# A hybrid attention and convolution block on one core: the conv result split behind the keys, its mean one block later, branch weights in pairs, branch groups in the attention's ramp, and the last tile in halves

## The chip, the cores and the metric

The kernel runs on one core of a Trainium2 chip. The metric is the device time of one execution in microseconds (us). TensorE (PE) does the matmuls, VectorE (DVE) and ScalarE (ACT) the elementwise work, GpSimd (POOL) some of it too, and SyncE (SP) issues the DMAs from one in-order queue.

## The reference, cut to what matters

Sequence 1024, model width 1024, float32, one layer.

```python
proj = rms_norm(x, norm_in_g) @ w_in
q, k, v, z_a, q_idx, k_idx, w_idx, glu_in, z_b, gate_a, gate_b = split(proj)
attn = sparse_attention(q, k, v, q_idx, k_idx, w_idx, rel_bias)   # top 256 keys of each query, 8 heads
y_a = (attn * silu(z_a)) @ w_branch_a
u = glu_in[:, :512] * sigmoid(glu_in[:, 512:])
c = silu(layer_norm(causal_depthwise_conv(u, conv_w, conv_b)))    # 31 taps
y_b = (c * silu(z_b)) @ w_branch_b
x = x + (sigmoid(gate_a) * y_a + sigmoid(gate_b) * y_b) @ w_out
x = x + sigmoid(rms_norm(x, ple_norm_g) @ w_ple_gate) * (p @ w_ple_proj)
out = rms_norm(x, final_norm_g)
```

## The kernel before

**Precision.** Every matmul operand is split into a high part and a low part (`hi`, `lo`), and `mm3` (L195) does three matmuls for each pair of operands (L199, L200, L201). A weight goes through `load_w` (L160): one DMA on SP into a `raw` buffer of 1024 words per partition (L173), a cast on ACT into `hi` (L177), a subtract on POOL into `lo` (L178). A weight with a per-row gain takes L182 and L183 instead. The value weights are 256 columns wide, so that one half of V takes two such loads.

**Order.** The program is written as a straight line, and a planner that simulates a timeline fixes each engine's order before the run. `hp()` raises an instruction's priority; `issue_after(i)` puts an instruction behind `i` on the engine of `i`. Buffers come from pools on a left and a right stack of SBUF; a pool that opens where an older one lay waits for that one's readers, tile by tile.

**Stages, in order.** The input is normalized and transposed into `hTh`, `hTl` (pool `h`). GLU, indexer scores (`wide`), then blocks of gate projections: `gate` (L455) runs, for each 128 columns of weight, two halves of 24 matmuls, an activation (L462) and a store (L463). Beside these, DVE does the conv taps (L295) and, with ACT, a bit search for each query's 256th score (L425 to L450), and then the masks (L506 to L521). The conv result `A[0..3]` gets a layer norm: a matmul with ones for the mean (L588), four gate blocks, a matmul for the variance (L601), then L604 to L618. After the masks `A` is split into `Yh` (ACT, L628) and `Yl` (DVE, L629), and pool `u`, which holds `A`, is closed. Four more gate blocks, `queries(m)` and `keys(m)` for m = 0 to 3 follow (each ends in stores of the split result to DRAM: L555, L556, L566, L567), then V: two halves c of 256 columns, eight tiles of 24 matmuls of 256 columns, evacuated by L650 and L651 into `VC`. The weights of half 0 come through pool `w3`, those of half 1 through pool `w`.

**Attention.** For each of 8 heads and 4 query pairs j: `scores` (matmuls L713, L714; mask add and row maximum on DVE, L721; exponential on ACT, L724), and two steps behind it `values` (transposes L773 to L781, split L784 and L785, matmuls L734). After every one of the 80 groups in `values`, `fill` may run one of 64 steps of `branch_b` (three matmuls of 512 columns, L812 to L814, all into PSUM bank 3; after every fourth a multiply, L817): the step of number n runs from group 4 + 1.25 n on. Branch b's weights come in single blocks of 128 columns through pool `wq` (three buffers of 512 words), which opens when V has ended.

**Last stages.** The merge (L860 to L874) multiplies the attention result by `w_branch_a`, block by block; the output projection takes `w_out` through pool `w2`; then the gate of the per-layer embedding (L947 to L960), the sums for the last norm (L962 to L968) and `final` (L935), which scales a tile in two halves (L938) and stores them (L939).

Of the kernel before, what the change touches and what calls it, by code (L numbers as in the profile page):

```python
# [38 lines left out]
def hybrid_block(ctx: ExitStack, tc: tile.TileContext, x, p, norm_in_g, w_in, conv_w, conv_b,  # L39
# [117 lines left out]

    wpools, wn = [WP], [0]

    def load_w(src, cols, nk_=NK, g=None, pool=None, prio=True):  # L160
# [428 lines left out]
    gate(C_SA, d_sa, 4, AF.Sigmoid)  # L589
# [51 lines left out]
    for c in range(2):  # L641
        w = load_w(win, [(C_V + 256 * c, 256)], pool=(WX, WP)[c])
# [50 lines left out]

    def scores(h, j, head):
# [4 lines left out]
        for i in (2 * j, 2 * j + 1):  # L699
# [10 lines left out]
            for a, b in pieces.get(n, ((0, n),)):  # L710
# [3 lines left out]
                nc.tensor.matmul(L, q_, kl[:, a:b], start=False, stop=True)  # L714
# [14 lines left out]
    FILL0, FILL1, PIN = 4, 1.25, True  # L729
# [65 lines left out]

    def branch_b():
        for m in range(8):
            for a in (m, m + 1):
                if a == 8:
                    waq[0] = load_w(wba, [(0, 128)], 4)  # L800
                elif a not in wbq:
                    wbq[a] = load_w(wbb, [(128 * a, 128)], 4)
            for hf in range(2):
# [4 lines left out]
                for k in range(4):  # L808
                    wh, wl = wbq[m][0][k], wbq[m][1][k]
                    pin = tc.issue_after(last_pe[0].ins) if PIN and last_pe[0] is not None else nullcontext()  # L810
                    with pin:
# [14 lines left out]
    def fill():  # L826
        while done[1] < 64 and done[0] >= FILL0 + FILL1 * done[1]:
# [32 lines left out]
    for m in range(8):  # L860
        wa = waq[m] if m in waq else load_w(wba, [(128 * m, 128)], 4)
# [3 lines left out]
        for hf in range(2):  # L865
# [3 lines left out]
            mm3(o, cut(wa, 0, 128), [(AH[k][:, sl], AL[k][:, sl]) for k in range(4)])  # L869
# [35 lines left out]
    for c in range(2):  # L905
        w = load_w(wo, [(512 * c, 512)], pool=W2)
# [123 lines left out]
```

## Time and profile before

| | us |
|---|---|
| median of three runs (1031.3 to 1032.18) | 1031.77 |
| the profiled execution | 1031.0 |
| its span, first to last instruction | 1029.1 |
| PE busy in the span | 998.2 (97%) |
| DVE, ACT, POOL busy | 714.7, 516.5, 277.3 |

PE is busy for nearly the whole span, but a busy PE isn't always PE at its higher clock: the granted clock says which of its two levels it had. The profiled execution took 1.9 us more than its span, and 0.77 us less than the median.

### The profile page before, as it was taken

To read this page: it belongs to the slowest core of one execution; us is meant where nothing else is said; L and a number is where in the kernel's file an instruction comes from. 1 tells how busy PE (TensorE), PEld (TensorE's weight loads), DVE (VectorE), ACT (ScalarE), POOL (GpSimd) and SP (SyncE) were. 2 spreads that over 40 slices of the span, in tenths; PEclk is the share of its full clock that TensorE was granted. 3 is DMA by queue.
4 is the path that set the end of the run, shared out by engine and by line. 5 is a ranking of instruction groups with operands and counts; after the bars stand their busy time and mean duration, and the time that the engine had idled before them with its cause. 6 is when DMAs were issued, how large, how long until landed. Compare 5 with 4: busy or idle time off the path is not lost.

```text
span 1029.1 us, 13977 instructions
## 1 busy us (share of the span) xinstructions
PE 998.2 (97%) x4993; PEld 835.3 (81%) x4993; DVE 714.7 (69%) x1418; ACT 516.5 (50%) x976; POOL 277.3 (27%) x260
## 2 busy tenths in 40 slices
PE   7999999999999999999997989999999999999996
PEld 6778888888888868788886979888888788888885
DVE  4396455899999999999795149898866922342443
ACT  7344444465665677776623157676643302351321
POOL 5231102321323111242204033444413713100011
PEclk9999999999999999999998999999999999999998
DMA  7240201142223242232447355565229552020012
GB/s 245 59 143 21 62 21 42 52 122 82 90 85 113 82 143 82 83 103 79 112 115 239 93 141 158 153 189 160 83 88 358 181 201 82 1 82 1 21 62 102
DMA packets 95203, 111.44 MB, mean 108 GB/s; under 512 B 6340, under 2 KB 64764, under 8 KB 95134
## 3 DMA queue, kind: packets, MB, share of 16 engines
q1 hardware_dynamic: 95134, 110.56, 35.3%
q8 instruction: 39, 0.64, 0.3%
q14 instruction: 30, 0.25, 0.1%
HBM read 81.16 MB, written 30.95 MB: 109 GB/s over the span
## 4 chain that ended last, share of the span: by engine, by line
PE 53%; DVE 35%; ACT 4%; issue 3%; DMA 3%; SPq 1%; POOL 0%; DVEq 0%; POOLq 0%; ACTq 0%
DVE acc L295 13%; PE bank L199 13%; PE bank L201 13%; PE bank L200 12%; PE bank L734 3%; DVE i_j L447 3%; DVE c_t L435 2%; DVE c_k L434 2%; DVE u_u L295 2%; ACT i_aj L429 2%; PE bank L773 2%; PE wide L371 1%; PE wide L372 1%; DMA w_raw<-in_w_in_dram 1%; PE bank L812 1%
## 5 line engine op out<-in xcount | busy, mean ns | idle before, releaser
L199 PE MATMUL bank<-h_h,w_hi 128*128 128x512 f32 (+2 forms) x720 | 279.8, 389 | 3.2 <-ACT s_g L281 1.2
L200 PE MATMUL bank<-h_l,w_hi 128*128 128x512 f32 (+2 forms) x720 | 278.4, 387 | 0.0
L201 PE MATMUL bank<-h_h,w_lo 128*128 128x512 f32 (+2 forms) x720 | 277.8, 386 | 0.0
L178 POOL TENSOR_TENSOR w_lo<-w_raw,w_hi 128x1024 fp32r<-128x1024 f32 (+1 forms) x57 | 141.6, 2487 | 353.2 <-ACT w_hi L177 344.9
L429 ACT ACTIVATE i_aj<-i_S,c_d 128x384 bf16<-128x384 f32 (+3 forms) x150 | 124.4, 829 | 79.1 <-DVE c_d L425 60.5
L199 PEld LDWEIGHTS bank<-h_h,w_hi 128*128 128x128 f32 (+1 forms) x720 | 134.9, 187 | 32.8 <-ACT s_g L281 1.6
L200 PEld LDWEIGHTS bank<-h_l,w_hi 128*128 128x128 f32 (+1 forms) x720 | 135.0, 188 | 28.0 <-issue 1.1
L201 PEld LDWEIGHTS bank<-h_h,w_lo 128*128 128x128 f32 (+1 forms) x720 | 134.9, 187 | 28.1 <-issue 1.2
L295 DVE SCALAR_TENSOR_TENSOR acc<-u_u,c_c,acc 128x1024 f32<-128x1024 f32 x100 | 128.7, 1287 | 2.4
L199 PE MATMUL bank<-w_hi,g_h 128*128 128x512 f32 x256 | 100.2, 393 | 0.0
L200 PE MATMUL bank<-w_lo,g_h 128*128 128x512 f32 x256 | 100.0, 393 | 0.0
L201 PE MATMUL bank<-w_hi,g_l 128*128 128x512 f32 x256 | 100.0, 391 | 0.0
L177 ACT CAST w_hi<-w_raw 128x1024 fp32r<-128x1024 f32 (+1 forms) x57 | 59.0, 1038 | 73.4 <-PE bank L201 28.3
L380 DVE SCALAR_TENSOR_TENSOR i_S<-wide,c_c,i_S 128x384 f32<-128x384 f32 (+5 forms) x42 | 39.4, 950 | 42.4 <-ACT wide L376 42.2
L704 POOL TENSOR_TENSOR e_mt<-m_m,ea_tp 128x256 f32<-128x256 bf16 (+1 forms) x64 | 41.1, 651 | 87.4 <-DVE c_c L721 73.4
L376 ACT ACTIVATE wide<-wide 128x384 f32<-128x384 f32 (+5 forms) x48 | 35.3, 743 | 47.4 <-PE wide L372 44.5
L199 PEld LDWEIGHTS bank<-w_hi,g_h 128*128 128x128 f32 x256 | 48.1, 188 | 9.8
L201 PEld LDWEIGHTS bank<-w_hi,g_l 128*128 128x128 f32 x256 | 48.1, 188 | 9.7
L200 PEld LDWEIGHTS bank<-w_lo,g_h 128*128 128x128 f32 x256 | 48.1, 188 | 9.7
L724 ACT ACTIVATE e_P<-e_P,c_c 128x384 f32<-128x384 f32 (+4 forms) x64 | 49.6, 776 | 11.0 <-DVE c_c L721 10.5
L959 DVE TENSOR_TENSOR s_g<-bank,s_g 128x512 f32<-128x512 f32 (+1 forms) x17 | 11.2, 661 | 63.0 <-ACT s_g L958 63.0
L199 PE MATMUL bank<-w_hi,h_h 128*128 128x256 f32 x128 | 37.1, 293 | 6.8 <-ACT w_hi L177 6.7
(239 smaller groups left out, 1920.4 us busy)
## 6 DMA issues: line engine op xcount, KB each, us to landing
w_raw<-in_w_in_dram SPq DMA_DIRECT2D x48, 512.0 KB, 4.1
x_x<-in_x_dram SPq DMA_DIRECT2D x8, 512.0 KB, 4.8
s_g<-d_sb SPq DMA_DIRECT2D x16, 256.0 KB, 4.7
ea_st<-d_q SPq DMA_DIRECT2D x8, 512.0 KB, 4.2
d_yb<-s_g SPq DMA_DIRECT2D x16, 256.0 KB, 2.1
f_sa<-d_sa SPq DMA_DIRECT2D x8, 512.0 KB, 5.7
f_yb<-d_yb SPq DMA_DIRECT2D x8, 512.0 KB, 6.8
w_raw<-in_w_out_dram SPq DMA_DIRECT2D x8, 512.0 KB, 3.8
```

What stands on the lines that cost most here:

```text
L177: nc.scalar.copy(hi, raw)
L178: nc.gpsimd.tensor_tensor(lo, raw, f(hi), op=OP.subtract)
L199: nc.tensor.matmul(o, lh, rh, start=(k == 0), stop=False)
L200: nc.tensor.matmul(o, lh, rl, start=False, stop=False)
L201: last_mm[0] = nc.tensor.matmul(o, ll, rh, start=False, stop=(k == n - 1))
L295: return nc.vector.scalar_tensor_tensor(o_, U[c][:, j:j + 1024], ccol[:, c, j:j + 1], i_, OP.mult, OP.add)
L376: nc.scalar.activation(d, d, AF.Relu)
L380: last_score = nc.vector.scalar_tensor_tensor(s_, d, wc, s_, OP.mult, OP.add)
L429: nc.scalar.activation(ajunk[:, :nblk[i]], sblk(i), AF.Sign, bias=f(cand)[:, i - 2:i - 1], accum_out=cnt[:, i - 2:i - 1])
L447: nc.vector.tensor_scalar(junk[:, :nblk[i]], sblk(i), f(cand)[:, i - 2:i - 1], 0.0, OP.is_ge, OP.add, accum_out=cnt[:, i - 2:i - 1])
L704: nc.gpsimd.tensor_tensor(mt, MK[:, moff[i] + n - wl:moff[i] + n], tp[:, 256 - wl:256], op=OP.add)
L724: nc.scalar.activation(P, P, AF.Exp, bias=init, scale=-1.0, accum_out=sm[:, c3])
```

## The change

The branch is the same arithmetic in another order.

1. **Mean one block later.** Gate block 0 of `C_SA` now stands ahead of the mean's matmul, and blocks 1 to 4 between mean and variance; blocks 5 to 7 follow later.
2. **Conv result split behind the keys.** `Yh` and `Yl` are made after the last key's evacuation, and pool `u` is closed there. Ahead of it the weights of V's half 0 are loaded, now through pool `w`; those of half 1 come through `w3`.
3. **Pool `w` is kept** to the end, at a place below `h`, with one `raw` buffer instead of two. Pool `wq` is gone. Branch weights come in pairs: 256 columns, 1024 words. The first two pairs are loaded ahead of the attention.
4. **Ramp.** In head 0 three, three, two and two steps of `branch_b` follow the scores of j = 0 to 3; the rest starts at group 6 with 1.2 groups to a step, so that the 64th comes with group 70 of 80.
5. **Merge.** Branch a's pairs 2 and 3 are loaded at m = 2 and m = 4, and the first load of `w_out` is put behind the last of them on POOL and SP.
6. **Last tile.** The 24 matmuls of the last tile become 24 of 256 columns for each half. The final gain is multiplied in early, the last sum is on DVE, the scale runs on ACT and DVE, one half each, and ACT issues one of the two stores. Squares are scaled by 1/32 inside the activation.

```diff
+RD = 1.0 / 32.0
+    WP = Pool("w", [("raw", 1024, 1), ("hi", 1024, 2), ("lo", 1024, 2)])
     HP = Pool("h", [("h0", 4096, 1), ("h1", 4096, 1), ("l0", 4096, 1), ("l1", 4096, 1)])
-    WP = Pool("w", [("raw", 1024, 2), ("hi", 1024, 2), ("lo", 1024, 2)])
...
     next_gate()
+    gate(C_SA, d_sa, 1, AF.Sigmoid)
     with hp(), tc.issue_after(last_mm[0].ins):
         for hf, sl, z0, z1, z2 in halves():
             nc.vector.tensor_tensor(z0, z0, A[3][:, sl], op=OP.add)
             nc.tensor.matmul(st[hf], ones, z0, start=True, stop=True)
-    gate(C_SA, d_sa, 4, AF.Sigmoid)
+    gate(C_SA, d_sa, 5, AF.Sigmoid, 1)
...
-    for c in range(4):
-        nc.scalar.copy(Yh[c], A[c])
-        nc.vector.tensor_tensor(Yl[c], A[c], f(Yh[c]), op=OP.subtract)
-    UP.close()
-    gate(C_SA, d_sa, 8, AF.Sigmoid, 4)
+    gate(C_SA, d_sa, 8, AF.Sigmoid, 5)
     for m in range(4):
         queries(m)
     for m in range(4):
         keys(m)
+    wv = load_w(win, [(C_V, 256)], pool=WP)
+    with tc.issue_after(last_kv[0].ins), tc.issue_after(last_kv[1].ins):
+        for c in range(4):
+            nc.scalar.copy(Yh[c], A[c])
+            nc.vector.tensor_tensor(Yl[c], A[c], f(Yh[c]), op=OP.subtract)
+    UP.close()
...
-        w = load_w(win, [(C_V + 256 * c, 256)], pool=(WX, WP)[c])
+        w = load_w(win, [(C_V + 256 * c, 256)], pool=WX) if c else wv
...
-    WP.close()
     HP.close()
-    WQ = Pool("wq", [("raw", 512, 3), ("hi", 512, 3), ("lo", 512, 3)])
-    wpools[0:] = [WQ]
+    wpools[0:] = [WP]
...
-    FILL0, FILL1, PIN = 4, 1.25, True
+    FILL0, FILL1 = 6, 1.2
+    RAMP = (3, 3, 2, 2)
...
+    def wb_load(q):
+        if q < 4:
+            wbq[q] = load_w(wbb, [(256 * q, 256)], 4)
+        else:
+            waq[q - 4] = load_w(wba, [(256 * (q - 4), 256)], 4)
+    wb_load(0)
+    wb_load(1)
...
+                        if c0 and hf:
+                            wb_load(q + 2)
...
-        while done[1] < 64 and done[0] >= FILL0 + FILL1 * done[1]:
+        while done[1] < 64 and done[0] >= FILL0 + FILL1 * (done[1] - sum(RAMP)):
...
             todo.append((h, j) + scores(h, j, head) + (ao,))
+            if h == 0:
+                for _ in range(RAMP[j]):
+                    next(fills)
+                done[1] += RAMP[j]
...
     for m in range(8):
-        wa = waq[m] if m in waq else load_w(wba, [(128 * m, 128)], 4)
+        if m in (2, 4):
+            wb_load(5 + m // 2)
+        wa = waq[m // 2]
...
     for c in range(2):
-        w = load_w(wo, [(512 * c, 512)], pool=W2)
+        with tc.issue_after(last_lo[0].ins) if c == 0 else nullcontext(), tc.issue_after(last_dma[0].ins) if c == 0 else nullcontext():
+            w = load_w(wo, [(512 * c, 512)], pool=W2)
...
-            nc.vector.scalar_tensor_tensor(o_, o_, r3[:, t:t + 1], FG[:, a:a + 512], OP.mult, OP.mult)
-            nc.sync.dma_start(out2d[t * 128:(t + 1) * 128, a:a + 512], o_)
+            if t < 7:
+                nc.vector.scalar_tensor_tensor(o_, o_, r3[:, t:t + 1], FG[:, a:a + 512], OP.mult, OP.mult)
+            elif a == 0:
+                nc.scalar.activation(o_, o_, AF.Copy, scale=r3[:, t:t + 1])
+            else:
+                nc.vector.tensor_scalar(o_, o_, r3[:, t:t + 1], None, OP.mult)
+            (nc.sync if t < 7 or a else nc.scalar).dma_start(out2d[t * 128:(t + 1) * 128, a:a + 512], o_)
...
-            mm3(o, mcut(t), cut(w, 0, 512))
...
+                if tail:
+                    o = bank((eb - 1 + a // part) % 8)
+                mm3(o[:, cc], mcut(t), cut(w, a, part))
...
+                if tail and a == 0:
+                    nc.vector.tensor_tensor(X2[:, t, 0:x0 + part], X2[:, t, 0:x0 + part], FG[:, 0:x0 + part], op=OP.mult)
...
-                nc.gpsimd.tensor_scalar(r3[:, t1], rx[:, t1], 1.0 / D, r2b[:, t1], OP.mult, OP.add)
+                nc.vector.tensor_scalar(r3[:, t1], rx[:, t1], r2b[:, t1], None, OP.add)
                 nc.gpsimd.tensor_tensor(r3[:, t1], r3[:, t1], nhalf, op=OP.pow)
+                if tail:
+                    nc.vector.tensor_tensor(xs, xs, FG[:, 768:1024], op=OP.mult)
```

## Rows read from the trace of the kernel before

**Rows 1.** The waits of PE over the whole span: who waited for whom, us in total, how often, the longest.
```profile
PE bank L199 <- ACT w_hi L177: 7.5, 2, 6.7
PE bank L588 <- DVE u_u L587: 2.5, 1, 2.5
PE bank L201 <- POOL wq_lo L178: 2.2, 1, 2.2
PE bank L734 <- ACT e_pth L784: 1.3, 1, 1.3
```

**Rows 2.** Busy time of each engine in slices of 25 us: an ordinary gate slice and two in which the granted clock (PEclk) falls. The columns are start:end, length, and busy us (instructions) of PE, PEld, DVE, ACT and POOL, then PEclk, DMA share and GB/s.
```profile
225.00:250.00 25.00, 25.00 (x112) 20.69 (x111) 24.37 (x26) 15.20 (x30) 6.04 (x3) 1.00 0.31 95
...
350.00:375.00 25.00, 22.52 (x89) 16.94 (x88) 24.05 (x49) 17.85 (x38) 5.81 (x3) 0.93 0.28 84
...
550.00:575.00 25.00, 18.27 (x137) 18.07 (x136) 5.38 (x11) 5.42 (x11) 4.93 (x3) 0.86 0.59 196
```

**Rows 3.** PE in order of time around the mean's and the variance's matmul: start, duration, operation. Matmuls overlap, so the pace is read from the starts.
```profile
364.25 0.39 PE L201 MATMUL bank<-h_h,w_lo 128*128 128x512 f32 x1
367.12 3.41 PE L588 MATMUL bank<-u_u,c_c 128*128 128x512 f32 x4 [2.48 <-DVE u_u L587]
...
370.75 0.49 PE L200 MATMUL bank<-h_l,w_hi 128*128 128x512 f32 x1
...
414.20 1.88 PE L601 MATMUL bank<-u_u,c_c 128*128 128x512 f32 x4
...
416.15 0.40 PE L200 MATMUL bank<-h_l,w_hi 128*128 128x512 f32 x1
```

**Rows 4.** DVE, POOL, SP and ACT in order of time between the split of the conv result and V's weights.
```profile
538.66 1.22 DVE L629 TENSOR_TENSOR y_y<-u_u,y_y 128x1024 fp32r<-128x1024 f32 x1
540.40 7.87 DVE L629 TENSOR_TENSOR y_y<-u_u,y_y 128x1024 fp32r<-128x1024 f32 x3
...
541.43 5.76 POOL L178 TENSOR_TENSOR w_lo<-w_raw,w_hi 128x1024 fp32r<-128x1024 f32 x2 [9.26 <-ACT w_hi L177]
...
541.80 0.32 SPq L566 DMA_DIRECT2D d_kh<-sx_g  x1
548.90 0.32 SPq L567 DMA_DIRECT2D d_kl<-s_g  x1
551.36 0.60 SPq L173 DMA_DIRECT2D w_raw<-in_w_in_dram  x1
...
556.73 1.04 ACT L177 CAST w_hi<-w_raw 128x1024 fp32r<-128x1024 f32 x1 [2.96 <-DMA w_raw<-in_w_in_dram]
```

**Rows 5.** Busy time and count of the instructions that read or write the weights' high parts, in V's first stretches after the wait (columns as in rows 2).
```profile
558.00:562.20 4.20, 4.13 (x15) 3.62 (x15) 0.00 (x0) 0.00 (x0) 2.22 (x1) 0.51 1.00 344
562.20:566.40 4.20, 4.13 (x24) 3.51 (x24) 0.00 (x0) 0.00 (x0) 0.00 (x0) 1.00 0.61 201
```

**Rows 6.** ACT's evacuation of a V tile: 2.51 us of waiting for PE and 0.37 us of work, from tile to tile.
```profile
576.78 0.37 ACT L650 CAST v_v<-bank 128x256 fp32r<-128x256 f32 x1 [2.51 <-PE bank L201]
```

**Rows 7.** The attention from the end of V on, in stretches of 14 us (columns as in rows 2), the first two and the last.
```profile
602.60:616.60 14.00, 10.97 (x60) 8.84 (x59) 10.49 (x45) 11.18 (x26) 8.71 (x12) 0.88 0.97 243
616.60:630.60 14.00, 14.00 (x92) 12.65 (x92) 12.89 (x48) 9.91 (x25) 4.47 (x9) 1.00 0.52 130
...
742.60:756.60 14.00, 14.00 (x94) 12.23 (x92) 10.78 (x29) 9.09 (x20) 1.12 (x1) 1.00 0.18 57
```

**Rows 8.** The first and the last matmul of one `branch_b` step on PE, and ACT's wait for branch b's first weights.
```profile
622.02 0.39 PE L812 MATMUL bank<-y_y,wq_hi 128*128 128x512 f32 x1
...
622.48 0.40 PE L814 MATMUL bank<-y_y,wq_lo 128*128 128x512 f32 x1
...
610.51 0.62 ACT L177 CAST wq_hi<-wq_raw 128x512 fp32r<-128x512 f32 x1 [2.06 <-DMA wq_raw<-in_w_branch_b_dram]
```

**Rows 9.** The merge: POOL's weight subtracts in order of time, PE's first matmul of the merge and its wait, and the stretch after the wait (last row, columns as in rows 2).
```profile
794.76 7.59 POOL L178 TENSOR_TENSOR w_lo<-w_raw,w_hi 128x1024 fp32r<-128x1024 f32 x2 [7.04 <-ACT w_hi L177]
802.32 5.09 POOL L178 TENSOR_TENSOR wq_lo<-wq_raw,wq_hi 128x512 fp32r<-128x512 f32 x3
810.95 2.39 POOL L178 TENSOR_TENSOR w_lo<-w_raw,w_hi 128x1024 fp32r<-128x1024 f32 x1 [3.54 <-ACT w_hi L177]
...
764.59 0.40 PE L199 MATMUL bank<-q_h,wq_hi 128*128 128x512 f32 x1
...
804.08 0.51 PE L201 MATMUL bank<-q_h,wq_lo 128*128 128x512 f32 x1 [2.18 <-POOL wq_lo L178]
...
804.10:808.40 4.30, 4.30 (x12) 3.40 (x13) 4.30 (x6) 0.62 (x1) 3.31 (x2) 0.60 0.76 247
```

**Rows 10.** The end, in order of time: PE's last matmul, then ACT, DVE and POOL; the last row is the output's stores (KB each, median us from issue to landing).
```profile
1020.04 0.39 PE L201 MATMUL bank<-w_hi,g_l 128*128 128x512 f32 x1
1020.47 0.84 ACT L958 ACTIVATE s_g<-bank,c_c 128x256 f32<-128x256 f32 x2 [3.84 <-PE bank L201]
1023.18 0.42 ACT L966 ACTIVATE o_j<-o_x 128x256 bf16<-128x256 f32 x1
1024.25 0.55 POOL L968 TENSOR_TENSOR c_c<-c_c 128x1 f32<-128x1 f32 x1
1024.83 1.42 DVE L938 SCALAR_TENSOR_TENSOR o_x<-o_x,c_c,o_fg 128x512 f32<-128x512 f32 x2 [1.08 <-POOL c_c L968]
...
out_dram<-o_x SPq DMA_DIRECT2D x16, 256.0 KB, 2.1
```

More of the change, by code (lines that the diff above doesn't have):

```diff
@@ L172, in load_w @@
             for c0, n in cols:
-                nc.sync.dma_start(raw[:, :, o:o + n], src[:, a:a + per, c0:c0 + n])
+                last_dma[0] = nc.sync.dma_start(raw[:, :, o:o + n], src[:, a:a + per, c0:c0 + n])
                 o += n
@@ L177, in load_w @@
                     nc.scalar.copy(hi, raw)
-                    nc.gpsimd.tensor_tensor(lo, raw, f(hi), op=OP.subtract)
+                    last_lo[0] = nc.gpsimd.tensor_tensor(lo, raw, f(hi), op=OP.subtract)
                 else:
@@ L235, in hybrid_block @@
     for t in range(8):
-        last_a = nc.scalar.activation(jk, xt[t], AF.Square, accum_out=rstat[:, t:t + 1])
-        nc.gpsimd.tensor_scalar(rx[:, t:t + 1], rstat[:, t:t + 1], 1.0 / D, EPS, OP.mult, OP.add)
+        last_a = nc.scalar.activation(jk, xt[t], AF.Square, scale=RD, accum_out=rstat[:, t:t + 1])
+        nc.gpsimd.tensor_scalar(rx[:, t:t + 1], rstat[:, t:t + 1], EPS, None, OP.add)
         last_p = nc.gpsimd.tensor_tensor(rx[:, t:t + 1], rx[:, t:t + 1], nhalf, op=OP.pow)
@@ L563, in keys @@
             with hp():
-                nc.scalar.copy(a_, o)
-                nc.vector.tensor_tensor(b_, o, f(a_), op=OP.subtract)
+                last_kv[0] = nc.scalar.copy(a_, o)
+                last_kv[1] = nc.vector.tensor_tensor(b_, o, f(a_), op=OP.subtract)
                 nc.sync.dma_start(d_kh[128 * m:128 * (m + 1), t0:t0 + 512], f(a_))
@@ L713, in scores @@
                 nc.tensor.matmul(L, q_, kh[:, a:b], start=True, stop=False)
-                nc.tensor.matmul(L, q_, kl[:, a:b], start=False, stop=True)
+                pin_at[0] = nc.tensor.matmul(L, q_, kl[:, a:b], start=False, stop=True)
                 for u, v_ in ((a, min(b, n - wl)), (max(a, n - wl), b)):
@@ L794, in hybrid_block @@
     wbq, waq = {}, {}
+    def wb_load(q):
[5 more added lines that the diff above has]
+    wb_load(1)
     def branch_b():
         for m in range(8):
[L798 to L802, printed above, removed]
+            q, c0 = m // 2, m % 2 * 128
             for hf in range(2):
@@ L808, in branch_b @@
                 for k in range(4):
-                    wh, wl = wbq[m][0][k], wbq[m][1][k]
-                    pin = tc.issue_after(last_pe[0].ins) if PIN and last_pe[0] is not None else nullcontext()
-                    with pin:
+                    wh, wl = wbq[q][0][k][:, c0:c0 + 128], wbq[q][1][k][:, c0:c0 + 128]
+                    with tc.issue_after(pin_at[0].ins):
                         nc.tensor.matmul(o, wh, Yh[k][:, sl], start=(k == 0), stop=False)
@@ L868, in hybrid_block @@
             fb += 1
-            mm3(o, cut(wa, 0, 128), [(AH[k][:, sl], AL[k][:, sl]) for k in range(4)])
+            mm3(o, cut(wa, m % 2 * 128, 128), [(AH[k][:, sl], AL[k][:, sl]) for k in range(4)])
             with hp():
@@ L949, in hybrid_block @@
             mm3(oe, [(PH[:, k, tt], PL[:, k, tt]) for k in range(2)], cut(we, 0, 512))
-            mm3(o, mcut(t), cut(w, 0, 512))
             s_ = stage()
             t1 = slice(t, t + 1)
-            part = 256 if t == 7 and c == 1 else 512
+            tail = t == 7 and c == 1
+            part = 256 if tail else 512
             for a in range(0, 512, part):
                 cc = slice(a, a + part)
-                xs = X2[:, t, 512 * c + a:512 * c + a + part]
+                x0 = 512 * c + a
+                xs = X2[:, t, x0:x0 + part]
+                if tail:
+                    o = bank((eb - 1 + a // part) % 8)
+                mm3(o[:, cc], mcut(t), cut(w, a, part))
                 with hp():
```

15 lines of the change are left out of this document (9 added, 6 removed).

## Prediction, written before the change was run

> **What bounds the kernel now.** The page was read first: PE is busy for 97% of the span, no other engine for more than 69%. So the time is PE's work plus the places where PE stands still or runs slowly, and the waits of PE say where it stands: 6.7 us for a cast of V's weights, 2.5 us for the sum ahead of the conv mean, 2.2 us for a low part of a merge weight, 1.3 us for a split in the attention [rows 1]. The slices of the span say what follows each wait. A gate slice holds 112 matmuls in 25 us, so 0.223 us for each of 512 columns; the slice with the mean holds 89 at a granted clock of 0.93 [rows 2]. Each long wait is paid twice: once standing, once at the lower of PE's two levels (1.2 instead of 2.4 GHz). The change touches every one of these places, so I cost it place by place and ask whether the cover it brings is ready in time.
>
> **Mean (part 1).** The last gate matmul before the mean starts at 364.25, so the next could start at 364.47. The mean starts at 367.12, and the second matmul behind it at 370.75; the same five steps around the variance take 416.15 - 414.20 = 1.95 [rows 3]. Lost: (367.12 - 364.47) + (370.75 - 367.12 - 1.95) = 4.3 us. Afterwards 48 gate matmuls, 10.7 us of work, stand between; DVE needs 2.5 us of them. Nothing follows the mean closely, as four blocks still lie between it and the variance. Gain 4.3, bounds 3.8 (half a microsecond of it kept at the new place) and 4.3.
>
> **V's weights (part 2).** DVE does three `Yl` subtracts in 7.87 us beside two POOL subtracts, where one alone took 1.22. A store of the low keys waits behind them on SP from 541.80 to 548.90, and the load of V's second weight half is queued behind that store and goes at 551.36; its cast begins at 556.73 [rows 4]. PE waits 6.7 us [rows 1] and then does 15 matmuls where it later does 24 in 4.2 us, at a clock of 0.51 [rows 5], which is another 9/24 x 4.2 = 1.6. Behind the keys the subtracts delay no store. V's half 0 now comes through pool `w`, whose two `hi` buffers were last read by keys 0 and 2, so the last cast may run one key block (10.7 us) before V begins; one load, cast and subtract took 8 us at most by the rows here (5.4 from issue to cast, then 2.4). Gain 8.3; bounds 5 (a wait of a third stays) and 8.3.
> What is late next: V's evacuation, since `VC` lies partly where `u` lay and must wait for the last subtract. Four of them at 7.87 / 3 take 10.5 us after the last key. V's tiles come every 2.51 + 0.37 = 2.88 us [rows 6] and have eight banks, 23 us, so it stays hidden; the cover is gone only if the split takes more than twice that long. The single `raw` buffer costs nothing in the gate blocks: pool `w3` has lived with one all along in the slice without a wait [rows 2]. At the start, where both GLU weights go through it, I allow 1 us either way.
>
> **Ramp (parts 3 and 4).** In the 14 us after V's end PE does 60 matmuls, in the next 14 us 92, at full clock [rows 7]. At that pace 60 take 9.1, so 4.9 us are lost. In this stretch ACT stands 2.06 us before the cast of branch b's first weights, which could only be asked for once V had ended [rows 8]; the pairs now come during V. The ten early steps bring 10 x 3 x 0.23 = 6.9 us of PE work [rows 8], enough to cover the loss, but they share one bank and need DVE for every fourth, and DVE is busy for 10.5 of the 14 us [rows 7]. Bounds 2 (ACT's wait alone) and 4.9; I take 4.0, near the top, since the work exceeds the hole.
> What is given back: the last ten groups have no steps. At 0.8 steps to a group that is 5.5 us of cover at most; the merge's first matmuls, which PE began at 764.59 [rows 9] before the last attention values, need only earlier heads and can take their place. Bounds 0 and -5.5; I take -0.5. Pairs cost ACT and POOL the same elements in half as many instructions; a POOL subtract of 1024 words (2.39 us alone [rows 9]) can now hold up a mask sum, which PE's steps cover.
>
> **Merge (part 5).** POOL does two `w_out` subtracts (3.8 us each beside a busy DVE) ahead of three small ones, and PE waits 2.2 us for one of these [rows 9]. Then it does 12 matmuls in 4.3 us instead of 4.3 / 0.223 = 19, so 1.6 more. Now the branch weights go first. Pair 2 needs the buffers of pair 0, free when m = 1 has ended, and has two blocks (10.7 us) for a cast and a subtract (1.0 + 3.8). Gain 3.8, bounds 0 (the wait moves, below) and 3.8.
>
> **Last tile (part 6).** From the end of PE's last matmul, 1020.43, to the span's end are 8.7 us. Sigmoid to last square takes 1023.18 - 1020.47 = 2.7 [rows 10] with both halves in it; with one half it is 0.42 and two DVE steps of about 0.4 (an estimate from 0.71 for 512 columns) and handovers, 1.4. The scale goes from 1.42 on DVE to 0.71 on two engines. One POOL hop less is worth some 0.2. The smaller matmuls cost 48 x 0.12 - 24 x 0.226 = 0.3. Gain 1.3 + 0.7 + 0.2 - 0.3 = 1.9; bounds 0.5 (the scale of tile 6, 1.42 on DVE, stands in the way) and 2.2.
>
> **Sum.** 4.3 + 8.3 + 4.0 - 0.5 + 3.8 + 1.9 = 21.8 us from the profiled execution's 1031.0 leave 1009.2. The median of the runs lies 0.77 above that execution, so I forecast 1010.0. By the lower bounds alone the gain would be 3.8 + 5 + 2 - 5.5 + 0 + 0.5 - 1 = 4.8, by the upper ones 24.5.
>
> **Rivals.**
> *The ramp and the merge keep their waits.* The softmax chain sets the ramp's pace, and the first `w_out` weights, now held back until the last branch weight is done, come late for the output projection. The merge lasts 8 x 24 x 0.223 = 42.8 us; pair 3 is free to be cast after half of it; then come 1 + 3.8 for the pair and four `w_out` subtracts of 3.8 [rows 9], 41.4 in all. The margin is 1.4, plus 4 because the last pair of rows is needed last. A load that lands 5 us late brings the wait back. For it speaks that POOL's subtracts are slow just there, against it that their mean over the run is nearer the 2.39 seen alone. Ramp 2, tail -2, merge 0: gain 4.3 + 8.3 + 0 + 0 + 1.9 = 14.5 and the time 1017.3.
> On POOL's pace beside DVE, the Trainium skill (SBUF — State Buffer, "Who interferes with whom") says that a VectorE instruction with two SBUF inputs and a GpSimd instruction that reads SBUF shut each other out for a whole instruction at a time. By that rule a subtract would be 2.39 plus whole DVE instructions of 0.7, some 3.1 to 3.8 us, which agrees with the 3.8 of the rows, and holding the four back into DVE's busiest stretch would speak against the change.
> *V's wait stays.* Half 0 still needs two loads through one `raw` buffer; if SP's order puts the second behind a key store again, the 8.3 stay: 1018.3. Against it: no subtract of the split stands before these stores any more.
> *Slower: ACT stands before pair casts.* Each pair is cast on ACT in the attention, in order, and with one `raw` buffer its load can't be issued before the previous pair's subtract. If the planner puts four of these casts ahead of the landing, ACT, and with it every exponential and split, stands for each. To turn the 21.8 us into a loss they must stand 5.5 us each; at 7.5 us each (a whole landing) the time is 1010.0 + 30 = 1040. Before, ACT stood so once, for 2.06 [rows 8], so this is unlikely.
> *No change.* The planner finds another order everywhere, and new small waits eat the gain: about 1031.
>
> **Chances.** A difference under 0.2% (2 us) is about what a measurement of this kernel can't tell from none. Forecast (1004.5 to 1014.5): 0.60. Ramp and merge keep their waits: 0.20. V's wait stays: 0.10. Slower by ACT's waits: 0.06. No change: 0.04. So faster 0.90, same 0.04, slower 0.06. The range holds the first case and most of the next two: 1004 to 1019; its lower end is the upper bounds (1031.8 - 24.5 = 1007.3) and 3 us for waits elsewhere that shift in our favour.
>
> **What would show it.** PE's waits no longer name L588 and no cast of V's weights over 1 us; the granted clock stays at 1.00 through the stretches of mean, V, ramp and merge; in the 14 us behind V some 85 matmuls; from PE's last matmul to the end under 7.2 us. The prediction is wrong if PE waits for `w_out` at the start of the output projection, for evacuated banks in V, or for splits in the attention's last ten groups.

## The result and the profile after

The changed kernel takes 1016.06 us (median of four runs, 1015.06 to 1016.99) against 1031.86 beside it: 0.9847 of the time, interval 0.983 to 0.9864. A second timing (e9 below) gave 0.9858 (0.984 to 0.9875). So 15.8 us were gained by the medians, 14.2 in the second timing, where 21.8 were forecast. The profiled execution has a span of 1013.3 us, 15.8 less than before.

PE's waits of over 1 us in total in the changed kernel (who waited for whom, us in total, times, longest), without those of the first 80 us. Its lines stand a little later than those of the kernel before: the three matmuls of `mm3` are L201, L202 and L203.

```profile
PE bank L203 <- POOL w_lo L180: 3.1, 2, 1.6
PE bank L202 <- POOL w_lo L180: 2.0, 1, 2.0
...
PE bank L201 <- ACT w_hi L179: 1.2, 1, 1.2
PE bank L720 <- DVE c_c L728: 1.2, 1, 1.2
```

The wait for the mean is gone [rows 1], and no split in the attention is waited for. But V's weights are still waited for (1.2 for a cast, then 2.0 for a subtract), and so are the merge's, 3.1 instead of 2.2. The 1.2 at the end, for a row maximum in the attention (at 689 us), is new.

Busy time in stretches of the changed kernel (columns as in rows 2): the mean, V's first matmuls, and twice 14 us from V's end.

```profile
350.00:375.00 25.00, 25.00 (x108) 20.06 (x107) 24.11 (x52) 16.51 (x35) 7.20 (x3) 1.00 0.31 95
...
544.00:548.00 4.00, 2.98 (x15) 2.98 (x16) 1.16 (x2) 2.03 (x3) 1.88 (x2) 0.68 0.94 330
548.00:552.00 4.00, 4.00 (x32) 4.00 (x31) 3.75 (x4) 3.29 (x4) 1.49 (x1) 0.90 1.05 388
...
591.00:605.00 14.00, 13.71 (x77) 11.63 (x75) 11.09 (x39) 7.86 (x18) 5.51 (x11) 1.00 0.25 81
605.00:619.00 14.00, 14.00 (x98) 12.89 (x97) 13.60 (x52) 11.06 (x27) 5.30 (x9) 1.00 0.62 157
```

At the mean PE keeps 1.00 (0.93 in rows 2), and in the ramp it does 77 and 98 matmuls at 1.00 (60 and 92 in rows 7). Of these places only V still drops to the lower level.

To see where the time went, the span is cut at four matmuls that both kernels have: the first on the conv weights, the first of V, the last of V, the first on `o_ph` (where the gate of the per-layer embedding begins). The numbers are differences of their starts in PE's timeline, in us; the first column counts from the span's start, the fifth to its end. e1 to e11 are the experiments below.

| kernel | to conv | to V | V | attention, merge, output | last part | span |
|---|---|---|---|---|---|---|
| before | 50.7 | 495.8 | 55.9 | 307.7 | 119.0 | 1029.1 |
| changed | 47.5 | 492.2 | 51.2 | 303.8 | 118.5 | 1013.3 |
| gained | 3.1 | 3.6 | 4.6 | 3.9 | 0.5 | 15.8 |
| forecast | 0 | 4.3 | 8.3 | 7.3 | 1.9 | 21.8 |
| e1 | 48.7 | 496.4 | 58.1 | 308.1 | 119.0 | 1030.3 |
| e2 | 49.4 | 492.2 | 46.0 | 304.3 | 118.5 | 1010.4 |
| e3 | 48.0 | 493.6 | 51.3 | 303.9 | 118.5 | 1015.2 |
| e4 | 48.5 | 492.3 | 52.4 | 304.9 | 119.2 | 1017.3 |
| e5 | 48.6 | 492.3 | 49.4 | 307.3 | 118.5 | 1016.0 |
| e6 | 47.6 | 492.2 | 56.6 | 303.7 | 118.5 | 1018.6 |
| e7 | 48.0 | 492.1 | 52.4 | 309.1 | 118.5 | 1020.1 |
| e8 | 47.6 | 493.6 | 52.4 | 304.8 | 118.5 | 1016.9 |
| e9 (changed, again) | 47.8 | 493.6 | 51.2 | 304.9 | 118.5 | 1016.0 |
| e10 | 47.9 | 492.3 | 50.9 | 302.8 | 118.5 | 1012.4 |
| e11 | 47.5 | 493.6 | 46.0 | 302.4 | 118.5 | 1007.9 |

The profiled executions of the changed kernel were the fastest of its four in the first timing and the slowest of its four in e9. They differ by 1.3 in the second and 1.2 in the fourth column: in e9 PE waits 1.15 us for VectorE's first step on the variance at 432 (as in e3, e8 and e11) and 1.30 at 818. The start is 47.5 to 49.4 in all executions with one `raw` buffer in pool `w`. V varies even where no edit touches it or what stands before it: with 2.9 to 3.8 us of waits for its weights it takes 49.4 at a granted clock of 1.00 (e5), 50.9 to 51.3 at 0.97 (the changed kernel, e3, e9, e10) and 52.4 at 0.93 (e4, e7, e8). So a column tells a difference of 1.5 us, and V's one of 3, only where its cause is seen in the rows; the last part tells 0.2.

### The profile page after: what moved, and what is told of

Same layout as the page of the kernel before. It is cut to its first block, busy times and chain, and to the rows that moved or that the text cites. A ratio compares the mean times of both kernels' runs of the same rounds, so it can differ in the third digit from the quotient of the medians.

```text
span 1013.3 us, 13955 instructions
## 1 busy us (share of the span) xinstructions
PE 990.4 (98%) x5017; PEld 832.7 (82%) x5017; DVE 712.3 (70%) x1427; ACT 515.6 (51%) x967; POOL 275.7 (27%) x242
## 5 line engine op out<-in xcount | busy, mean ns | idle before, releaser
L201 PE MATMUL bank<-h_h,w_hi 128*128 128x512 f32 (+2 forms) x720 | 278.4, 387 | 1.4 <-DVE h_l L257 1.0
L202 PE MATMUL bank<-h_l,w_hi 128*128 128x512 f32 (+2 forms) x720 | 277.6, 386 | 0.0
L203 PE MATMUL bank<-h_h,w_lo 128*128 128x512 f32 (+2 forms) x720 | 277.3, 385 | 0.0
L180 POOL TENSOR_TENSOR w_lo<-w_raw,w_hi 128x1024 fp32r<-128x1024 f32 x67 | 168.8, 2524 | 378.0 <-ACT w_hi L179 347.1
L201 PEld LDWEIGHTS bank<-h_h,w_hi 128*128 128x128 f32 (+1 forms) x720 | 134.5, 187 | 29.9 <-DVE h_l L257 1.2
L203 PEld LDWEIGHTS bank<-h_h,w_lo 128*128 128x128 f32 (+1 forms) x720 | 134.5, 187 | 27.8 <-issue 0.6
L202 PEld LDWEIGHTS bank<-h_l,w_hi 128*128 128x128 f32 (+1 forms) x720 | 134.6, 187 | 27.5 <-issue 0.5
L179 ACT CAST w_hi<-w_raw 128x1024 fp32r<-128x1024 f32 x67 | 69.7, 1041 | 84.6 <-PE bank L203 25.4
L202 PE MATMUL bank<-w_lo,g_h 128*128 128x512 f32 (+1 forms) x264 | 101.6, 386 | 0.0
L203 PE MATMUL bank<-w_hi,g_l 128*128 128x512 f32 (+1 forms) x264 | 101.4, 385 | 0.0
L201 PE MATMUL bank<-w_hi,g_h 128*128 128x512 f32 (+1 forms) x264 | 100.9, 385 | 0.0
L731 ACT ACTIVATE e_P<-e_P,c_c 128x128 f32<-128x128 f32 (+3 forms) x64 | 49.6, 777 | 16.0 <-DVE c_c L728 15.8
L202 PEld LDWEIGHTS bank<-w_lo,g_h 128*128 128x128 f32 x264 | 49.6, 188 | 9.5
L203 PEld LDWEIGHTS bank<-w_hi,g_l 128*128 128x128 f32 x264 | 49.7, 188 | 9.4
L201 PEld LDWEIGHTS bank<-w_hi,g_h 128*128 128x128 f32 x264 | 49.6, 188 | 9.5
L449 DVE TENSOR_SCALAR_CACHE_REDUCE i_j<-i_S,c_d 128x896 bf16<-128x896 f32 (+1 forms) x36 | 43.4, 1206 | 0.0
```

What stands on the lines that cost most here:

```text
L180: last_lo[0] = nc.gpsimd.tensor_tensor(lo, raw, f(hi), op=OP.subtract)
L201: nc.tensor.matmul(o, lh, rh, start=(k == 0), stop=False)
L202: nc.tensor.matmul(o, lh, rl, start=False, stop=False)
L203: last_mm[0] = nc.tensor.matmul(o, ll, rh, start=False, stop=(k == n - 1))
L449: nc.vector.tensor_scalar(junk[:, :nblk[i]], sblk(i), f(cand)[:, i - 2:i - 1], 0.0, OP.is_ge, OP.add, accum_out=cnt[:, i - 2:i - 1])
L731: nc.scalar.activation(P, P, AF.Exp, bias=init, scale=-1.0, accum_out=sm[:, c3])
```

## Experiments

The ratios are to the kernel before on the same chip; 0.001 is 1 us.

**The start (e1).** In the kernel before: `WP = Pool("w", [("raw", 1024, 2), ...` with 1 for 2.

> The kernel before with one change: pool w has one raw buffer instead of two. In the trace of the changed kernel the start is 3.1 us shorter up to the first matmul on the conv weights (50.68 to 47.54), which the prediction had allowed 1 us either way. Theory: the single raw buffer does it. The second full GLU load is then asked for behind the small conv weights and the 72-column load, which is the one that PE waits for; expected: that matmul at 47.5 to 48.0, PE's two waits of 0.78 and 1.18 us at 24 to 27 gone, the granted clock 1.00 there, and 1028.7 us. Rival: the start is shorter for another edit (the square's scale and the shorter POOL step); then nothing moves here, 1031.9 us. What the single buffer does to V's weights in the old order is open, up to 3 us either way.

Measured: 1.0003 (0.9994 to 1.0012). The start is 2.0 us shorter, with a clock of 1.00 from 24 to 32 (0.78 and 0.80 before), so the theory holds there; in the old order the same edit makes V 2.3 longer (waits of 8.9 in it instead of 7.2), and nothing is left. PE's waits at the two places in e1:

```profile
25.72 0.45 PE L199 MATMUL bank<-h_h,w_hi 128*72 128x512 f32 x1 [0.26 <-ACT s_g L281]
...
558.09 0.80 PE L199 MATMUL bank<-w_hi,h_h 128*128 128x256 f32 x2 [8.39 <-ACT w_hi L177]
```

With one buffer the second full GLU load can't be asked for at 7.3 us; the casts of the 72-column load and of the one behind it come 0.5 us sooner on ScalarE, and PE's wait of 1.18 at 26.2 is 0.26.

**V's weights (e2, e6).** e2 gives each half of V two raw buffers:

```diff
+            if pair:
+                pool = pair[i_ % 2]
...
-    wv = load_w(win, [(C_V, 256)], pool=WP)
+    wv = load_w(win, [(C_V, 256)], pool=WP, pair=(WP, WX))
```

> The changed kernel, but each half of V's weights takes its first load through pool w and its second through pool w3, so that two raw buffers serve the half that PE needs first. Theory: V still loses 5.3 us because the second load of half 0 could only be asked for once the first one's subtract had ended, and so stood on SP behind a query store (which waited for DVE until 530.67) and four key stores, until 535.08. Expected: that load goes at about 531.9, its cast ends by 537.5, its subtract by 540, before PE asks at 541.2; PE's waits for V's weights (1.2 and 2.0 us) and the half clock behind them are gone, 1010.9 us. Rival: the loads are late because the transfers are slow just there; then the wait stays and the time is 1015 to 1016. Second rival: the time saved comes back as a wait in the attention's first groups: 1013 to 1016.

Measured: 0.9819 (0.9806 to 0.9832), V 46.0 instead of 51.2, no wait in it and a clock of 1.00. Of these 5.2 us the ratios show 2.9 to 4.0: the start of the profiled execution is 1.9 longer than the changed kernel's, and a wait of 0.6 for a row maximum comes back at the start of the attention. e6 puts the split back (the same lines behind the keys go):

```diff
+    for c in range(4):
+        nc.scalar.copy(Yh[c], A[c])
+        nc.vector.tensor_tensor(Yl[c], A[c], f(Yh[c]), op=OP.subtract)
+    UP.close()
     gate(C_SA, d_sa, 8, AF.Sigmoid, 5)
```

> The changed kernel with the split of the conv result at its old place, ahead of the last gate blocks. Theory of the prediction: the split in the keys' stretch was what held the stores and with them V's loads; undone, V takes 56 to 58 us instead of 51.2 (the kernel before, and the kernel before with one raw buffer) and the time is 5 to 7 us longer, 1021 to 1023. Rival: in the changed kernel the second load of half 0 is late for the index search on VectorE and the one raw buffer, whatever the split does; then V stays within 1.5 us of 51.2 and the time within 1.5 of 1016.

Measured: 0.9908 (0.9894 to 0.9921), V 56.6. Both theories hold: the split behind the keys is worth 5.4 us of V here (PE's waits in V are 7.5 with it at the old place and 3.3 in the changed kernel, the rest is clock), and a second raw buffer takes away the 5.2 that stay. Here is the path in the changed kernel, VectorE, SP, ScalarE and PE in order of time:

```profile
529.97 0.67 DVE L555 SCALAR_TENSOR_TENSOR sx_g<-bank,s_g 128x512 fp32r<-128x512 f32 x1
530.67 1.08 SPq L558 DMA_DIRECT2D d_q<-sx_g  x2
531.85 0.54 SPq L175 DMA_DIRECT2D w_raw<-in_w_in_dram  x1
...
535.08 1.08 SPq L175 DMA_DIRECT2D w_raw<-in_w_in_dram  x1
...
541.50 1.04 ACT L179 CAST w_hi<-w_raw 128x1024 fp32r<-128x1024 f32 x1 [1.78 <-DMA w_raw<-in_w_in_dram]
...
542.60 0.38 PE L201 MATMUL bank<-w_hi,h_h 128*128 128x256 f32 x1 [1.23 <-ACT w_hi L179]
545.02 0.38 PE L202 MATMUL bank<-w_lo,h_h 128*128 128x256 f32 x1 [2.04 <-POOL w_lo L180]
```

The load at 531.85 is for V's second half, through pool `w3`; the one at 535.08 is the second for the first half, which PE wants at 541.4. Its raw buffer was free at 526.6, but a query store ahead of it on SP waited for a subtract that came at 529.97 in the middle of the index search on VectorE, and four key stores stood in between. In e2 the two loads change places, and in e6 the old obstacle is back: three `Yl` subtracts hold the key's low part, its store and the load behind it.

```profile
532.48 7.89 DVE L635 TENSOR_TENSOR y_y<-u_u,y_y 128x1024 fp32r<-128x1024 f32 x3
...
540.99 0.32 SPq L571 DMA_DIRECT2D d_kl<-s_g  x1
541.40 0.39 SPq L175 DMA_DIRECT2D w_raw<-in_w_in_dram  x1
...
547.05 0.58 PE L201 MATMUL bank<-w_hi,h_h 128*128 128x256 f32 x1 [5.63 <-ACT w_hi L179]
```

**The ramp (e5).** `FILL0, FILL1 = 4, 1.25` and `RAMP = (0, 0, 0, 0)` in the changed kernel.

> The changed kernel without the early steps of branch b: RAMP all zero, FILL0 and FILL1 as before (4 and 1.25); the pairs of weights, kept and preloaded, stay. By the traces V's end to the merge's last matmul took 212.3 us before and 207.9 after; in the first 20 us of it 8.7 us went beyond the matmuls' own pace before and 3.4 after. Theory: the early steps cover the ramp, worth 5.2 us, and 1 to 2 us of it are given back between 680 and 770, where no steps are left; undone, V's end to the merge's end becomes 211 to 212 and the time 3 to 4 us longer than the changed kernel's 1016, 1019 to 1020. Rival: half of the ramp's gain came from the weights that wait ready; then the loss is 2 or less, 1018. Second rival: the steps missing at the end cost as much as the ramp gains: no difference, 1016.

Measured: 0.9881 (0.9867 to 0.9894), by the ratios 2.4 to 3.5 us more than the changed kernel's two timings, and the fourth column is 2.4 to 3.5 longer. What goes beyond the matmuls' own pace in the first 20 us behind V (each matmul's distance to the next, less the median of its shape: 0.227 for 512 columns, 0.120 for 256, 0.109 for 128) is 6.1 before, 2.8 here and 0.8 in the changed kernel. So the preloaded pairs closed 3.3 of the hole and the early steps 2.0: the first rival is right about the ramp, and the sum lies between it and the theory. The rest of e5's loss lies behind the ramp: three waits of 1.1 us for attention outputs (at 647, 687 and 728). And its merge, with PE's steps in another order, has no wait for a pair, but two for VectorE stand behind it, 1.0 and 2.2.

**The merge (e3, e7, e8, e10).** e3 casts and subtracts the last two pairs in halves of 128 columns; e7 drops `issue_after(last_lo)` and `issue_after(last_dma)` from the first `w_out` load; e8 moves subtracts to VectorE:

```diff
-                    last_lo[0] = nc.gpsimd.tensor_tensor(lo, raw, f(hi), op=OP.subtract)
+                    last_lo[0] = (nc.vector if dve else nc.gpsimd).tensor_tensor(lo, raw, f(hi), op=OP.subtract)
```

> The changed kernel, but the last two pairs of branch a's weights are cast and split in two halves of 128 columns each (the same load, the same elements, twice the instructions). Theory: the merge keeps 3.1 us of waits (1.62 at 776.3, 1.51 at 789.9) because PE finishes the first pairs early and all at once, so that a pair's cast and subtract (1.05 and 2.75 us) have less than 4 us and not two blocks of 10.7 us. With halves the first half is ready 1.4 to 1.9 us sooner: the first wait gone, the second under 0.5 us, 1013 to 1013.5 us. Rival: VectorE, which is busy for all of 788 to 804, sets the merge's end; then PE's waits shrink, but the output projection starts no earlier: 1016.

Measured: 0.986 (0.9847 to 0.9873), no gain. The first wait falls to 0.69, the second stays at 1.65, and PE waits 1.40 for VectorE behind the merge. Whether the halves put it there isn't settled: that wait is 0.15 in one execution of the changed kernel and 1.30 in the other (e9). The gain that the theory promised didn't come.

> The changed kernel with the first w_out loads no longer held behind the last branch weight. Theory: the two w_out subtracts (3.4 us each beside VectorE's work) come ahead of the last pair's or the last two pairs' on GpSimd; PE's waits in the merge grow from 3.1 us to 6 or more, and the time to 1019 or more. Rival: GpSimd stands idle for 8.8 us ahead of the last pair's subtract, so the w_out subtracts fit in there and slow only VectorE: PE's waits stay at 3 us, 1015 to 1017.

Measured: 0.9919 (0.9906 to 0.9933), the fourth column 4.2 to 5.4 longer than in the two executions of the changed kernel: holding `w_out` back is worth that much. PE's waits in the merge grow to 1.63 and 2.34 only, 4.0 and not 6; the rest is a granted clock of 0.72 from 790 to 796, and 1.26 and 1.64 us for VectorE behind the merge. The 2.34 are for a cast, third in line behind two casts of `w_out`, so it is ScalarE's order as much as GpSimd's.

> The changed kernel, but the low parts of branch a's last two pairs and of w_out's first half are subtracted on VectorE instead of GpSimd. In the changed kernel's merge VectorE's sums and subtracts with both inputs in SBUF take 0.68 us alone and 1.8 to 2.7 beside a GpSimd subtract, and the subtracts take 3.4 instead of 2.4, so that VectorE is busy for all of 776 to 813; the halved pairs had only moved PE's wait behind the merge. Theory: six subtracts of 1.22 us on VectorE (1.22 as the split of the conv result took alone) cost 7.3 us there and give back some 12; PE's wait for the first late pair falls from 1.62 to under 0.3 us and the second from 1.51 to under 0.5, VectorE has caught up by 806 instead of 813, and the time is 2.5 to 3 us less, 1013. Rival: VectorE's own queue now delays the last pairs, since it works in order; then PE's waits grow and the time is 1016 to 1019.

Measured: 0.9878 (0.9865 to 0.9892), no gain; the rival holds. But what the theory started from, VectorE's loss beside GpSimd, is seen. VectorE's groups from 776 to 813, first of the changed kernel, then of e8 (line, operation, count, busy us, mean ns):

```profile
L894 DVE TENSOR_TENSOR g_l<-f_sa,g_h 128x512 fp32r<-128x512 f32 x16 | 17.7, 1114 | 0.5 <-ACT g_h L893 0.3
L892 DVE TENSOR_TENSOR f_sa<-f_sa,f_yb 128x512 f32<-128x512 f32 x14 | 14.6, 1064 | 0.0
L891 DVE TENSOR_TENSOR f_sa<-bank,f_sa 128x512 f32<-128x512 f32 x14 | 8.9, 675 | 0.0
```

```profile
L892 DVE TENSOR_TENSOR f_sa<-f_sa,f_yb 128x512 f32<-128x512 f32 x16 | 10.5, 678 | 0.0
L894 DVE TENSOR_TENSOR g_l<-f_sa,g_h 128x512 fp32r<-128x512 f32 x14 | 10.4, 749 | 0.0
L891 DVE TENSOR_TENSOR f_sa<-bank,f_sa 128x512 f32<-128x512 f32 x16 | 10.2, 676 | 0.0
L180 DVE TENSOR_TENSOR w_lo<-w_raw,w_hi 128x1024 fp32r<-128x1024 f32 x6 | 7.3, 1212 | 5.5 <-ACT w_hi L179 5.5
```

The 11 us that VectorE loses beside GpSimd are saved and 7.3 are spent on the subtracts. The rest is lost in VectorE's order: it stands 5.5 us for the cast of the first late pair, with the merge's next products behind that subtract, and PE now waits 1.94 for one of them. VectorE has 48 steps in this merge, at some 0.64 us each 31 us, and can begin with most of them only when the last attention values are there. That led to e10, which puts two matmuls of the last group earlier:

```diff
+        if h == 7 and j == 3:
+            with hp():
+                for e in range(2):
+                    nc.tensor.transpose(R[:, 128 * e:128 * e + 128], rb[:, e, :, :], ident)
         nc.scalar.copy(ar, O[64:128])
```

> The changed kernel with one thing put earlier: for the last group of attention values the two matmuls that spread the row sums (L751 of the changed kernel) come right behind the last product with V instead of 4.8 us later. In the changed kernel the last product starts at 761.93, these two at 767.08, and the last attention output, on which a quarter of every merge sum waits, is complete only at 771.3; VectorE, which is then busy for all of 776 to 813, stands 4.2 us for them. Theory: VectorE and the late weight pairs are about 4 us earlier against PE's work; PE's waits in the merge (1.62 and 1.51 us) fall to under 1 us together, V's end to the merge's end becomes 205 to 206 instead of 207.9, and the time is 2 to 3 us less than the changed kernel beside it. Rival: the pairs' chain (release by PE, cast, subtract, one raw buffer) sets the pace whatever VectorE does; then the waits stay and the gain is under 0.5.

Measured: 0.9844 (0.9829 to 0.9859), by the medians 2.2 us less than e9 beside it, by the ratios 1.4, and the two intervals overlap: the time alone doesn't settle it. The fourth column is 302.8, 1.0 to 2.1 less than in the changed kernel's executions; the first wait stays at 1.64, the second becomes 0.84 and 0.37, and behind the merge 0.35 for a low part of `w_out` stands in place of 1.30 for VectorE in e9. Between theory and rival: where VectorE was late the waits fall, but the first late pair has its own cause. These are the rows of the changed kernel, PE, ScalarE and GpSimd:

```profile
761.93 0.52 PE L742 MATMUL bank<-e_d,v_v 128*128 128x256 f32 x3
...
767.08 0.38 PE L751 MATMUL bank<-c_c,e_rb 128*128 128x128 f32 x2
...
772.37 1.05 ACT L179 CAST w_hi<-w_raw 128x1024 fp32r<-128x1024 f32 x1 [2.43 <-PE bank L202]
773.50 2.75 POOL L180 TENSOR_TENSOR w_lo<-w_raw,w_hi 128x1024 fp32r<-128x1024 f32 x1 [2.19 <-ACT w_hi L179]
785.09 10.37 POOL L180 TENSOR_TENSOR w_lo<-w_raw,w_hi 128x1024 fp32r<-128x1024 f32 x3 [8.84 <-ACT w_hi L179]
...
776.30 0.50 PE L203 MATMUL bank<-q_h,w_lo 128*128 128x512 f32 x1 [1.62 <-POOL w_lo L180]
789.89 0.50 PE L203 MATMUL bank<-q_h,w_lo 128*128 128x512 f32 x1 [1.51 <-POOL w_lo L180]
```

The cast at 772.37 waits for PE to let go of pair 0's buffer, and PE needs the new pair at 774.7, 2.3 us later. The second pair's load can't go before the first one's subtract has freed the only raw buffer, at 776.25.

**The last tile (e4).** `final` and the last loop as in the kernel before.

> The changed kernel with the last tile as in the kernel before (part 6 undone). The traces say: from PE's last matmul to the end 8.7 us before and 7.9 after, so 0.8 gained, while the stretch from the output projection's first matmul to PE's last took 205.6 before and 206.3 after, so 0.8 lost. By this reading the time stays within 0.5 of the changed kernel, 1015.6 to 1016.5. By the prediction's sum (1.9 gained by part 6) it would be 1018.

Measured: 0.9879 (0.9865 to 0.9894), 2 to 3 us above the changed kernel's two timings, which by itself would fit the prediction's sum; but of the span's 4.0 us only 0.7 are in the last part, and the rest are 0.9 of start, 1.2 in V (52.4, as in e7 and e8) and a wait of 1.31 behind the merge, which e9 has without this edit. In all ten profiles with the new last tile the last part takes 118.5 us, in the three with the old one 119.0 to 119.2. So part 6 is worth 0.5 to 0.7, near the expectation's reading and not the prediction's 1.9.

**All together (e9, e11).** e9 is the changed kernel again, for a baseline on the same chip.

> The changed kernel once more, beside the two that follow on the same chip. Expected by the earlier timing: 0.983 to 0.986 of the kernel before; V 51 to 52.5 us, the merge's two waits 1.6 and 1.5 us.

> The changed kernel with two raw buffers for V's first half (as in the earlier run), the early matmuls of the run above, and the last group's product and subtract on VectorE instead of GpSimd (1.29 us each there). If the gains add: 5.3 from V, 2 to 3 from the merge, about 1 from the faster last group: 8 to 9 us less than the changed kernel beside it, near 1007. If the merge gives nothing, 5 less, near 1011.

Measured: e9 0.9858 (0.984 to 0.9875), with V 51.2 and the merge's two waits 1.63 and 1.50, as expected; e11 0.9797 (0.9782 to 0.9813), 1009.92 us against 1016.9, 7.0 less, between the two cases that were expected. In the spans it is 8.1: 5.2 from V, 2.5 from the fourth column, 0.4 from the start. It is the fastest kernel here. Beside e10's early matmuls it has the last group's product and subtract on VectorE, so its merge doesn't test either alone. What waits remain in its merge, on PE:

```profile
771.30 0.50 PE L205 MATMUL bank<-q_h,w_lo 128*128 128x512 f32 x1 [0.33 <-POOL w_lo L182]
783.70 0.50 PE L205 MATMUL bank<-q_h,w_lo 128*128 128x512 f32 x1 [1.23 <-POOL w_lo L182]
809.06 0.50 PE L204 MATMUL bank<-w_lo,g_h 128*128 128x512 f32 x1 [0.53 <-POOL w_lo L182]
```

## Why the prediction was right or wrong

The sign and the range held; the sum was 6 us too large, and its parts did worse than the sum. In part that is luck: 3.1 of the 15.8 us came from the start, where nothing was forecast. Without them the time would be some 1019, at the range's upper end.

Of the signs that the prediction named, three came: no wait for the mean's sum, a clock of 1.00 at mean, ramp and merge, and none of the waits that would have made it wrong. Three did not: V still waits 1.2 for a cast and the clock falls there, the first 14 us behind V hold 77 matmuls and not 85, and from PE's last matmul to the end are 7.9 us, not under 7.2.

- **Mean: right.** Forecast 4.3, gained 3.6. The mean's four matmuls start at 372.90 and take 1.88 us, as the variance's do [rows 3], and the next gate matmul follows at once. The missing 0.7 are two waits of 0.33 and 0.42 us at 73 and 75 us, where the conv's inputs are now wanted earlier (e1, with the earlier start alone, has them too). In e9 the wait of 1.15 at 432 takes another 1.2, so that 2.2 are left.
- **V's weights: the right cause, half of the size.** That the subtracts held the store and the load is shown by e6 (5.4 us). The step that failed is "one load, cast and subtract took 8 us at most", counted from the last buffer's release: the load was asked for only at 535.08, 6.3 us before it was needed, since SP's order and the single raw buffer put it behind stores, one of which waited for a query's subtract. And from there to the end of the subtract (544.97) it took 9.9, not 8. That was the rival "V's wait stays", priced as all or nothing. Against e2's 46.0, V lost 9.9 in the kernel before (8.3 were priced) and loses 5.2 now, 3.3 of it standing. By e2 none need have stayed.
- **Ramp: right in sum.** Forecast 4.0 - 0.5 = 3.5. By the pace of the matmuls the changed kernel loses 9.4 us from V's end to 180 us later and the kernel before 13.8, so 4.4 were gained: 5.3 in the first 20 us, over the upper bound of 4.9, less 0.9 behind them, where the wait of 1.2 at 689 is new. Its lower bound, 2 for ScalarE's wait alone, was small: 3.3 of the 5.3 are the pairs' readiness, 2.0 the early steps. The stretch without steps at the end cost no visible wait.
- **Merge: wrong.** Forecast 3.8, gained nothing (in the 40 us that follow both lose 4.1). The failed step is that pair 2 "has two blocks (10.7 us)". Of the 96 matmuls on pairs 0 and 1, PE's order has 54 ahead of the last product with V and 21 more ahead of the two matmuls at 767.08; only 21 are left for the time after the last attention output, 21 x 0.227 = 4.8 us for both pairs together. So from pair 0's release to pair 2's first use are 2.3 us, and cast and subtract take 3.9. The rival "ramp and merge keep their waits" came true for the merge, though not through `w_out`; its guard, the holding back, is worth 4.2 to 5.4 us (e7). Nor did the working price VectorE in the merge: where the waits for pairs shrink or go (e8, e5), waits for VectorE stand in their place.
- **Last tile: mis-sized.** Forecast 1.9, gained 0.5. ScalarE, VectorE and GpSimd at the end of the changed kernel:

```profile
1005.47 0.47 ACT L988 ACTIVATE s_g<-bank,c_c 128x256 f32<-128x256 f32 x1 [0.43 <-PE bank L203]
1006.95 0.42 ACT L998 ACTIVATE o_j<-o_x 128x256 bf16<-128x256 f32 x1 [1.01 <-DVE o_x L990]
1006.78 1.41 DVE L960 SCALAR_TENSOR_TENSOR o_x<-o_x,c_c,o_fg 128x512 f32<-128x512 f32 x2
1008.10 0.20 DVE L999 TENSOR_SCALAR c_c<-c_c 128x1 f32<-128x1 f32 x1
1009.10 0.72 ACT L962 ACTIVATE o_x<-o_x,c_c 128x512 f32<-128x512 f32 x1 [1.64 <-POOL c_c L1000]
```

  From sigmoid to last square 1.5 instead of 2.7, as forecast. But the sum on VectorE stands behind tile 6's scale (the bound that the prediction named and did not take) until 1008.10, 0.6 late, and from the last scale's end (1009.82) to the span's end it takes 3.5 instead of 1029.1 - 1026.25 = 2.85. PE's stretch is 0.4 longer, as forecast (0.3).
- **Start: not forecast.** 3.1 us were gained where the prediction allowed 1. e1 shows 2.0 of them for the single raw buffer; with starts of 47.5 to 49.4 in the executions that have it, whether another edit gives the rest isn't shown.

The rival of ACT standing before pair casts didn't come true: of the four pair casts inside the attention three wait for nothing and the last 0.34 us for PE.

## What to carry to other kernels

A load's cover is counted from when its queue can issue it: list what stands ahead of it on that queue, and which engine each of those waits for. Where one engine works ahead on part of every block, buffers that were freed block by block come free all at once; the cover is then the time of the remaining work only. When a wait is removed on the engine that sets the time, look whether another engine is busy throughout that stretch: here VectorE was, neither halved nor moved subtracts gained anything, and letting VectorE start sooner gave back one to two us (e10).

## What the hardware showed beside this

Beside a GpSimd subtract, VectorE's steps with both inputs in SBUF can take far longer, and those that read a PSUM bank don't. From the changed kernel's merge, during GpSimd's three subtracts (3.46 us each on average, where one alone takes 2.40):

```profile
785.09 4.75 POOL L180 TENSOR_TENSOR w_lo<-w_raw,w_hi 128x1024 fp32r<-128x1024 f32 x1 [8.84 <-ACT w_hi L179]
...
786.33 0.68 DVE L892 TENSOR_TENSOR f_sa<-f_sa,f_yb 128x512 f32<-128x512 f32 x1
786.93 0.68 DVE L894 TENSOR_TENSOR g_l<-f_sa,g_h 128x512 fp32r<-128x512 f32 x1
787.96 2.43 DVE L894 TENSOR_TENSOR g_l<-f_sa,g_h 128x512 fp32r<-128x512 f32 x1 [0.35 <-ACT g_h L893]
790.31 1.28 DVE L891 TENSOR_TENSOR f_sa<-bank,f_sa 128x512 f32<-128x512 f32 x2
791.51 4.50 DVE L892 TENSOR_TENSOR f_sa<-f_sa,f_yb 128x512 f32<-128x512 f32 x2
795.93 0.68 DVE L894 TENSOR_TENSOR g_l<-f_sa,g_h 128x512 fp32r<-128x512 f32 x1
```

The two products from a bank take 0.64 each, the two sums 2.25 each. The first subtract shows the other direction: while VectorE goes on with two-input steps that keep their 0.68, up to 787.6, the subtract lasts 4.75; the next such step, behind a gap of 0.35, then takes 2.43. The Trainium skill (SBUF — State Buffer, "Who interferes with whom") says that a VectorE instruction with two SBUF inputs contends with a GpSimd instruction that reads SBUF, that one with at most one SBUF input doesn't (outside the two-port modes), and that the shared ports are an exclusive lock. The trace agrees, in both directions.

The second surprise is what a wait costs behind it. The merge's waits of 1.6 and 1.5 us left the granted clock at 1.00, and so did the 1.2 at 689 us; V's 1.2 and 2.0, with one matmul between them, were followed by 4 us at 0.68 and 4 at 0.90. In the kernel before, 2.2 us in the merge were followed by 0.60 [rows 9]. But the wait's length doesn't tell it alone. These are the first 16 us of V in e5, e10 and e7, with waits of 0.89 and 2.05, 0.93 and 2.04, 1.28 and 2.04 (columns as in rows 2):

```profile
540.81:556.81 16.00, 13.06 (x106) 12.66 (x105) 9.50 (x12) 8.73 (x13) 4.86 (x3) 1.00 0.95 328
...
540.15:556.15 16.00, 13.03 (x93) 12.63 (x92) 8.98 (x11) 8.47 (x12) 5.04 (x3) 0.89 0.98 330
...
540.11:556.11 16.00, 12.68 (x81) 12.28 (x80) 9.19 (x11) 8.45 (x12) 4.94 (x3) 0.79 0.96 327
```

Nearly the same waits cost no clock in e5 (106 matmuls), some in e10 (93) and more in e7 (81). What decides it isn't shown here.
